# Hybrid decoder step on one core: retention state updates whose operands are stacked on TensorE, with cross products gathered in one tile and new states made in rounds

## The chip, the cores and the metric

One core of one Trainium2 chip runs the whole layer in one launch. The metric is the device time of that launch in microseconds (us), the median of several runs. TensorE (PE in the profile) multiplies matrices, PEld is its loading of weights, DVE is VectorE, ACT is ScalarE, POOL is GpSimd and SP is the engine that issues most loads.

## What is computed

One layer of a hybrid decoder works on 256 prompt tokens of one sequence and on 8 new tokens of each of 8 sample sequences (320 tokens in all, width 2048, float32). The lines that matter here are those of the retention mixer, per head (4 heads, 256 wide), for the sample sequences:

```
scores  = einsum('bhid,bhjd->bhij', q, k) * decay          # new tokens among themselves
o_inner = einsum('bhij,bhje->bhie', scores, v)
o_cross = einsum('bhid,bhde->bhie', q, S) * q_dec          # new tokens against the old state
S_new   = gamma**C * S + einsum('bhjd,bhje->bhde', k * k_dec, v)
```

S is a 256 x 256 state for each of 8 sequences and 4 heads. C is 8 for the sample sequences. A pooling mixer, an output projection and a SwiGLU feed-forward network follow. Outputs are y for all tokens and the new states.

## The kernel before

All activations are kept transposed (features on partitions, 320 tokens along the free axis). A float32 product is made of float32r products: each operand is split into a high part (a ScalarE cast, L152) and a low part (a VectorE subtraction, L155), and three products are summed (L160 hi*hi, L161, L162). `project` runs one projection of 16 feature tiles by 4 output blocks: 192 matmuls of 128x320 into four PSUM accumulators (`acc_...` in the profile). For each head there are two projections (`acc_qk`, `acc_vg`), then come two for the pooling mixer (`acc_u`), four for the output (`acc_wo`) and those of the feed-forward network (`acc_gu`, `acc_dn`).

Between the matmuls of a projection stand the small stages of a head: transposes (`tps`, `tpk`, `tvs`, `tpv`), scores (`sc`, `scs`), outputs (`o`), cross products with the old state (`cr`, L418), the final prompt state (`st`), new sample states (`ns`, L538), sample outputs (`os`, L552 and L553) and the gate (`on`). They take PSUM from a pool of three banks (`aux`). A list scheduler fixes each engine's order when the program is built, and each engine then runs its own instructions in that order.

For the samples of a head the new k and v (64 tokens on 64 partitions) are split into halves in `smp`. A state update of the sequence pair `bp` wants a stack of 32 rows (high and low halves of k against those of v, for 8 tokens) on its own quarter of the partitions, `kv[32*bp : 32*bp + 32]`. Before, this was made by a trip through DRAM: four writes of `smp` to `kv_d` and four loads of `kv` on POOL's queue. Then `new_state(bp)` makes four matmuls with 32 contraction rows (two sequences `b`, two halves `t`) and VectorE adds the decayed state (L541). The cross products `cr` write 16 partitions for each pair; a ScalarE scaling, a write to `x_d` and one load bring them together in `cx`, which `sample_outputs` multiplies by a 0/1 table `sel`. The other product of `sample_outputs` has 64 contraction rows (`vs_f`, `sds`).

Of the kernel before, what the change touches and what calls it, by code (L numbers as in the profile page):

```python
# [24 lines left out]
P = 128  # L25
# [37 lines left out]
N_CON = _at  # L63


def _constants():
# [12 lines left out]
    i = np.arange(TP)[None, :]  # L79
    for h in range(H):  # L80
        mask[h, :, P:] = np.where(i >= j, np.exp((i - j) * lg[h]), 0.0) * ks
        a = CON["mask_s"][0] + TS * h
        sj = np.arange(TS)[:, None]
        si = np.arange(TS)[None, :]
        ok = (sj % NB == si % NB) & (si >= sj)
        con[:TS, a : a + TS] = np.where(ok, np.exp((si - sj) // NB * lg[h]), 0.0) * ks
        for t in range(2):
            con[:, CON["kdec"][0] + 2 * h + t] = np.exp((TP - 1 - (np.arange(P) + P * t)) * lg[h]) * ks
        con[:TS, CON["kdec_s"][0] + h] = np.exp((NS - 1 - np.arange(TS) // NB) * lg[h]) * ks
        con[:16, CON["qdec"][0] + h] = np.exp((np.arange(16) % NS + 1) * lg[h])  # L90
# [6 lines left out]
    return trig, con.astype(f32), mask.astype(f32), decay  # L97
# [3 lines left out]
def layer_kernel(ctx, tc, x, vec, trig, con, mask, pool_in, s_ret, w_in, w_pool, w_out, w_gu, w_dn,  # L101
# [7 lines left out]
    dram = ctx.enter_context(tc.tile_pool(name="dram", bufs=4, space=bass.MemoryType.DRAM))  # L109
# [170 lines left out]
    with ExitStack() as ret_ctx:  # L280
# [129 lines left out]
        def cross(h, bp, q_s, x_d):  # L410
# [4 lines left out]
            for b in range(2):  # L415
                for t in range(2):
                    for n_, s_ in enumerate((lo, hi)):
                        nc.tensor.matmul(ps[:16, b * DK : b * DK + DK],  # L418
                                         q_s[:, t, 2 * bp + b].rearrange("p s j -> p (s j)"),
                                         s_[:, b, t * DK : t * DK + DK],  # L420
                                         start=t == 0 and n_ == 0, stop=t == 1 and n_ == 1)
            cr = rp.tile([16, 2, DK], F32, tag="cr", name=f"cr_sb{h}_{bp}")
            nc.scalar.mul(cr, ps[:16].rearrange("p (b e) -> p b e", b=2), cst("qdec", h, 1, 16))
            nc.gpsimd.dma_start(out=x_d[2 * bp : 2 * bp + 2].rearrange("b r e -> r b e"), in_=cr)

        def head(h, accs_qk, project_vg):
# [7 lines left out]
            x_d = dram.tile([NB, 16, DK], F32, tag="x_d", name=f"x_d{h}")  # L434
            kv_d = dram.tile([4, NS, NB, 2, DK], F32R, tag="kv_d", name=f"kv_d{h}")
            smp = rp.tile([TS, 2, 2, DK], F32R, tag="smp", name=f"smp{h}")
            ktok = keep.tile([P, 2, 2, DK], F32R, tag="ktok", name=f"ktok{h}")
            q_s = rp.tile([P, 2, NB, 2, NS], F32R, tag="q_s", name=f"q_s{h}")
# [3 lines left out]
            sds = rp.tile([TS, TS], F32, tag="sds", name=f"sds{h}")  # L442
# [22 lines left out]
            def k_sample():  # L465
# [3 lines left out]
                split2_scaled(smp[:, 1, 0], smp[:, 1, 1], ps[:TS, :DK], cst("kdec_s", h, 1, TS))  # L469
                for t in range(2):  # L470
                    qt = q_r[:, t, TP:].rearrange("p (j b) -> p b j", b=NB)
                    split2(q_s[:, t, :, 0], q_s[:, t, :, 1], qt)

            def sample_scores():
# [20 lines left out]
            vs_f = rp.tile([TS, DK], F32, tag="vs_f", name=f"vs_f{h}")  # L495
            o_t = t640(f"o_t{h}")
            kv = rp.tile([P, 2, 2, DK], F32R, tag="kv", name=f"kv{h}")

            def v_sample():
# [3 lines left out]
                nc.vector.tensor_copy(vs_f, ps[:TS, :DK])  # L503
# [7 lines left out]
            def kv_load(bp):  # L511

                nc.gpsimd.dma_start(out=kv[32 * bp : 32 * bp + 32],
                                    in_=kv_d.rearrange("q j b a e -> (q j) b a e")[:, 2 * bp : 2 * bp + 2])
# [18 lines left out]
            def new_state(bp):  # L533
                raw, ks = s_raws.pop(4 * h + bp), slice(32 * bp, 32 * bp + 32)
                for b in range(2):
                    ps = aux(f"ns{h}_{bp}_{b}")
# [4 lines left out]
                    nc.vector.scalar_tensor_tensor(sl, sl, decay[h], ps.rearrange("p (t e) -> p t e", t=2),  # L541
                                                   op0=ALU.mult, op1=ALU.add)
                nc.gpsimd.dma_start(out=o_rs[h, bp], in_=raw)
                s_load(4 * h + bp + 4)

            def sample_outputs():
                cx = rp.tile([P, DK], F32, tag="cx", name=f"cx{h}")
                nc.gpsimd.dma_start(out=cx, in_=x_d.rearrange("b r e -> (b r) e"))
# [5 lines left out]
                nc.scalar.copy(o_t[:, :, TP:], ps[:, : 2 * TS].rearrange("p (e t) -> p e t", e=2))  # L554
# [387 lines left out]
```

## Time and profile before

| | |
|---|---|
| three runs | 1435.94, 1436.27 (median), 1436.89 us |
| the profiled execution's own time | 1435.48 us |
| its span, first to last instruction | 1433.7 us |
| PE busy | 1409.2 us, 98% |
| DVE busy | 751.5 us, 52% |
| ACT busy | 578.5 us, 40% |
| POOL busy | 63.6 us, 4% |

The span and the 1.8 us around it make the profiled execution's time. A matmul's listed duration is longer than its distance to the next one, since matmuls overlap in the array; what a matmul costs TensorE is read from start to start.

### The profile page before, as it was taken

How to read it: one execution, taken by the hardware profiler on the slowest of the kernel's cores; microseconds unless marked ns; L12 is line 12 of the kernel's file. 1: busy time of each engine (PE TensorE's matmuls, PEld its weight loads, DVE VectorE, ACT ScalarE, POOL GpSimd, SP SyncE). 2: the span in 40 equal slices, each digit the busy share in tenths (PEclk: the TensorE clock that was granted, in tenths of full speed). 3: DMA queues.
4: the chain of work that ended last, by engine and by line, in shares of the span. 5: the costliest groups of instructions: out<-in, count | busy, mean ns of one | idle time of the engine just before them, and what ended most of it. 6: DMA issues, size and time to landing. Idle time of an engine off the chain costs nothing.

```text
span 1433.7 us, 22936 instructions
## 1 busy us (share of the span) xinstructions
PE 1409.2 (98%) x9578; PEld 1390.9 (97%) x9578; DVE 751.5 (52%) x1003; ACT 578.5 (40%) x751; POOL 63.6 (4%) x122
## 2 busy tenths in 40 slices
PE   8999999999999999999999999999999999999995
PEld 8999999999999989999999999999999999999995
DVE  7657575758644674444334444444544444454455
ACT  6445454545444353333333333223333323333352
POOL 1020202021000000000000000000000000000000
PEclk9999999999999999999999999999999999999998
DMA  9484747575564145544444444444454444444442
GB/s 335 134 258 145 237 166 239 169 237 159 173 235 150 57 148 170 156 153 153 148 148 147 150 148 158 148 147 149 151 155 149 147 147 153 153 149 148 147 133 74
DMA packets 69368, 233.84 MB, mean 163 GB/s; under 512 B 8368, under 2 KB 10864, under 8 KB 69264
## 3 DMA queue, kind: packets, MB, share of 16 engines
q1 hardware_dynamic: 58608, 204.28, 44.5%
q0 software_dynamic: 10080, 27.44, 6.1%
q8 instruction: 75, 1.23, 0.3%
q10 hardware_dynamic: 576, 0.66, 0.1%
q14 instruction: 29, 0.24, 0.0%
HBM read 216.28 MB, written 16.05 MB: 162 GB/s over the span
## 4 chain that ended last, share of the span: by engine, by line
PE 95%; DVE 3%; ACT 1%; DMA 0%; issue 0%; DVEq 0%; ACTq 0%; POOLq 0%
PE acc_gu L162 14%; PE acc_gu L160 14%; PE acc_gu L161 14%; PE acc_dn L160 7%; PE acc_dn L162 7%; PE acc_dn L161 7%; PE acc_vg L161 3%; PE acc_vg L162 3%; PE acc_wo L162 3%; PE acc_vg L160 3%; PE acc_wo L161 3%; PE acc_wo L160 3%; PE acc_qk L160 3%; PE acc_qk L161 3%; PE acc_qk L162 2%; PE acc_u L160 1%
## 5 line engine op out<-in xcount | busy, mean ns | idle before, releaser
L160 PE MATMUL acc_gu<-hf_h,hi_gu 128*128 128x320 f32 x1312 | 405.5, 309 | 0.2 <-ACT hi_gu L152 0.2
L161 PE MATMUL acc_gu<-hf_l,hi_gu 128*128 128x320 f32 x1312 | 405.1, 309 | 0.0
L162 PE MATMUL acc_gu<-hf_h,lo_gu 128*128 128x320 f32 x1312 | 403.0, 309 | 1.9 <-DVE lo_gu L155 1.9
L155 DVE TENSOR_TENSOR lo_gu<-raw_gu,hi_gu 128x1024 fp32r<-128x1024 f32 x166 | 203.1, 1223 | 270.3 <-ACT hi_gu L152 270.3
L152 ACT CAST hi_gu<-raw_gu 128x1024 fp32r<-128x1024 f32 x166 | 174.1, 1049 | 336.2 <-PE acc_gu L161 300.1
L162 PEld LDWEIGHTS acc_gu<-hf_h,lo_gu 128*128 128x128 f32 x1312 | 245.6, 188 | 2.7 <-DVE lo_gu L155 2.7
L160 PEld LDWEIGHTS acc_gu<-hf_h,hi_gu 128*128 128x128 f32 x1312 | 246.3, 188 | 0.6 <-ACT hi_gu L152 0.5
L161 PEld LDWEIGHTS acc_gu<-hf_l,hi_gu 128*128 128x128 f32 x1312 | 246.3, 188 | 0.1
L161 PE MATMUL acc_dn<-a_l,hi_dn 128*128 128x320 f32 x704 | 217.3, 309 | 0.0
L160 PE MATMUL acc_dn<-a_h,hi_dn 128*128 128x320 f32 x704 | 217.3, 309 | 0.0
L162 PE MATMUL acc_dn<-a_h,lo_dn 128*128 128x320 f32 x704 | 215.4, 309 | 0.0
L155 DVE TENSOR_TENSOR lo_dn<-raw_dn,hi_dn 128x1024 fp32r<-128x1024 f32 x88 | 107.7, 1224 | 137.8 <-ACT hi_dn L152 137.7
L152 ACT CAST hi_dn<-raw_dn 128x1024 fp32r<-128x1024 f32 x88 | 92.2, 1048 | 183.0 <-PE acc_dn L161 153.3
L160 PEld LDWEIGHTS acc_dn<-a_h,hi_dn 128*128 128x128 f32 x704 | 132.2, 188 | 0.0
L161 PEld LDWEIGHTS acc_dn<-a_l,hi_dn 128*128 128x128 f32 x704 | 132.2, 188 | 0.0
L162 PEld LDWEIGHTS acc_dn<-a_h,lo_dn 128*128 128x128 f32 x704 | 131.6, 188 | 0.0
L152 ACT CAST hi_in<-raw_in 128x1024 fp32r<-128x1024 f32 (+1 forms) x82 | 83.8, 1026 | 96.9 <-PE acc_qk L161 48.4
L155 DVE TENSOR_TENSOR lo_in<-raw_in,hi_in 128x1024 fp32r<-128x1024 f32 (+1 forms) x82 | 97.7, 1194 | 46.4 <-ACT hi_in L152 45.4
L161 PE MATMUL acc_vg<-xw_l,hi_in 128*128 128x320 f32 x256 | 79.8, 312 | 0.0
L161 PE MATMUL acc_wo<-mi_l,hi_wo 128*128 128x320 f32 x256 | 79.0, 309 | 0.0
L160 PE MATMUL acc_vg<-xw_h,hi_in 128*128 128x320 f32 x256 | 78.8, 310 | 0.0
L162 PE MATMUL acc_vg<-xw_h,lo_in 128*128 128x320 f32 x256 | 78.7, 309 | 0.0
(351 smaller groups left out, 2057.0 us busy)
## 6 DMA issues: line engine op xcount, KB each, us to landing
raw_gu<-in_w_gu SPq DMA_DIRECT2D x168, 512.0 KB, 3.5
raw_dn<-in_w_dn SPq DMA_DIRECT2D x88, 512.0 KB, 3.6
raw_in<-in_w_in SPq DMA_DIRECT2D x78, 512.0 KB, 4.4
raw_wo<-in_w_out SPq DMA_DIRECT2D x32, 512.0 KB, 3.6
s_raw<-in_s_ret POOLq DMA_DIRECT2D x16, 512.0 KB, 5.8
out_rs<-s_raw POOLq DMA_DIRECT2D x16, 512.0 KB, 5.4
x_t<-in_x SPq DMA_DIRECT2D x8, 320.0 KB, 4.0
kv_d<-smp POOLq DMA_DIRECT2D x16, 128.0 KB, 4.9
```

The costliest lines, as they stand in the source:

```text
L152: nc.scalar.copy(hi[:, ks], src[:, ks])
L155: nc.vector.tensor_tensor(lo[:, ks], src[:, ks], hi[:, ks].bitcast(F32), op=ALU.subtract)
L160: nc.tensor.matmul(ps, wh, xh, start=start, stop=False)
L161: nc.tensor.matmul(ps, wh, xl, start=False, stop=False)
L162: nc.tensor.matmul(ps, wl, xh, start=False, stop=stop)
```

## The change

- `smp` now holds the high halves on partitions 0 to 63 and the low halves on 64 to 127. The new function `stacked` multiplies it by a 0/1 table `part` (two matmuls for k, two for v), and ScalarE copies the result to `kv`. `kv_d`, its writes and its loads are gone. The table (256 KB) is loaded by SP at the start and cast by ScalarE once.
- `cross` writes 32 partitions of one PSUM tile for a pair (the stationary q gets zero columns for the other sequence), and ScalarE scales it straight into its quarter of `cx`. `x_d`, its writes and the load of `cx` are gone.
- `vs_f` and `sds` have 128 partitions, the upper 64 zero, so all four products of `sample_outputs` have 128 contraction rows.
- `new_states` replaces `new_state`: a round takes up to three (pair, sequence) items with a PSUM bank for each, and issues the `t=0` products of all of them, then the `t=1` products. The first product of a round waits by an added dependency for the last two evictions ahead of it. Three rounds for a head: sequence 0 of pairs 0 to 2, sequence 1 of pairs 0 to 2, both sequences of pair 3. Sample outputs and gate stand between the rounds; the prompt's final state comes last.
- `vs_f`, `q_s`, `sds` become tiles for the whole run, cleared by three VectorE memsets at the start.

```diff
+    part = np.zeros((P, 2, 2, P), f32)
+    for a in range(2):
+        low = r // (NS << a) % 2
+        for b in range(2):
+            part[TS * low + r % NS * NB + r // 32 * 2 + b, a, b, r] = 1.0
...
+    vs_f = keep.tile([P, DK], F32, name="vs_f")
+    nc.vector.memset(vs_f, 0.0)
+    q_s = keep.tile([P, 2, 4, 4, 2, NS], F32R, name="q_s")
+    nc.vector.memset(q_s.bitcast(F32), 0.0)
+    part = keep.tile([P, 2, 2, P], F32R, name="part")
+    sds = keep.tile([P, TS], F32, name="sds")
+    nc.vector.memset(sds, 0.0)
...
-                        nc.tensor.matmul(ps[:16, b * DK : b * DK + DK],
-                                         q_s[:, t, 2 * bp + b].rearrange("p s j -> p (s j)"),
+                        nc.tensor.matmul(ps[:32, :DK],
+                                         q_s[:, t, bp, 2 * b : 2 * b + 2].rearrange("p c s j -> p (c s j)"),
                                          s_[:, b, t * DK : t * DK + DK],
-                                         start=t == 0 and n_ == 0, stop=t == 1 and n_ == 1)
-            cr = rp.tile([16, 2, DK], F32, tag="cr", name=f"cr_sb{h}_{bp}")
-            nc.scalar.mul(cr, ps[:16].rearrange("p (b e) -> p b e", b=2), cst("qdec", h, 1, 16))
-            nc.gpsimd.dma_start(out=x_d[2 * bp : 2 * bp + 2].rearrange("b r e -> r b e"), in_=cr)
+                                         start=b + t + n_ == 0, stop=b + t + n_ == 3)
+            nc.scalar.mul(cx[32 * bp : 32 * bp + 32], ps[:32, :DK], cst("qdec", h, 1, 32))
+        def stacked(kv, a, smp, name):
+            ps = aux(f"tp{'vk'[a]}r{name}")
+            for b in range(2):
+                nc.tensor.matmul(ps[:, b * DK : b * DK + DK], part[:, a, b], smp[:, a], start=True, stop=True)
+            nc.scalar.copy(kv[:, :, a], ps.rearrange("p (b e) -> p b e", b=2))
...
-                split2(smp[:, 0, 0], smp[:, 0, 1], ps[:TS, :DK])
-                for q in range(4):
-                    both = smp.rearrange("p a s e -> p (a s) e")[:, q % 2 : 3 + q // 2 : 2 + q // 2 - q % 2]
-                    nc.gpsimd.dma_start(out=kv_d[q].rearrange("j b a e -> (j b) a e"), in_=both)
-                for bp in range(4):
-                    kv_load(bp)
+                split2(smp[:TS, 0], smp[TS:, 0], ps[:TS, :DK])
...
+            def new_states(some):
+                pss = [aux(f"ns{h}_{bp}_{b}") for bp, b in some]
+                def product(i, t):
+                    (bp, b), ps = some[i], pss[i]
+                    ks = slice(32 * bp, 32 * bp + 32)
+                    return nc.tensor.matmul(ps[:, t * DK : t * DK + DK], kv[ks, b, 1, t * P : t * P + P],
+                                            kv[ks, b, 0, :], start=True, stop=True).ins
+                i0 = 0 if evicted else len(some) - 1
+                start = product(i0, 0)
+                for e in evicted[-2:]:
+                    tc.add_manual_dep(start, e.name, SYNC, reason="a round at a time")
+                with tc.issue_after(start):
+                    for t in range(2):
+                        for i in range(len(some)):
+                            if t or i != i0:
+                                product(i, t)
...
+            rounds = [[(bp, 0) for bp in range(3)], [(bp, 1) for bp in range(3)], [(3, 0), (3, 1)]]
...
-            return [v_sample, v_tokens, outputs] + state + [lambda: cross(h, 3, q_s, x_d)] + [
-                lambda bp=bp: new_state(bp) for bp in range(4)] + [sample_outputs, gate]
+            return [v_sample, v_tokens, v_stacked, outputs, lambda: cross(h, 3, cx), lambda: new_states(rounds[0]),
+                    sample_outputs, lambda: new_states(rounds[1]), gate, lambda: new_states(rounds[2])] + state
```

What the scheduler makes of it is seen on TensorE in head 0, where the new states stand among the matmuls of head 1's `acc_qk` (192 in all). In `ns_2_0_1025` the first number is the pair, the second the sequence, and the third only a buffer number. Before:

```order
L538 MATMUL ns_0_0_1043<-kv_851 128x256 x2
L538 MATMUL ns_0_1_1047<-kv_851 128x256 x2
L538 MATMUL ns_1_0_1054<-kv_851 128x256 x2
...
L538 MATMUL ns_1_1_1058<-kv_851 128x256 x2
...
L538 MATMUL ns_2_0_1095<-kv_851 128x256 x2
...
L538 MATMUL ns_2_1_1099<-kv_851 128x256 x2
...
L538 MATMUL ns_3_0_1136<-kv_851 128x256 x2
L538 MATMUL ns_3_1_1140<-kv_851 128x256 x2
L160 MATMUL acc_qk_0_852<-xw_h,hi_in_4_969 128x320
```

And now, the first two rounds with the sample outputs between them:

```order
L550 MATMUL ns_2_0_1025<-kv_501 128x256
L550 MATMUL ns_0_0_1023<-kv_501 128x256
L550 MATMUL ns_1_0_1024<-kv_501 128x256
L550 MATMUL ns_0_0_1023<-kv_501 128x256
L550 MATMUL ns_1_0_1024<-kv_501 128x256
L550 MATMUL ns_2_0_1025<-kv_501 128x256
...
L577 MATMUL os_1035<-sds,vs_f 128x64
L578 MATMUL os_1035<-con_t,cx_500 128x64
L577 MATMUL os_1035<-sds,vs_f 128x64
L578 MATMUL os_1035<-con_t,cx_500 128x64
...
L550 MATMUL ns_0_1_1071<-kv_501 128x256
```

Five groups of `ns`, after 96, 118, 121, 123 and 144 matmuls of the projection, have become three, after 96, 142 and 173, with four products of pair 3 in the last. The sample outputs moved from 145 to 120, the gate's `on` from 177 to 166. The new `stacked` products for v stand after 67 (the transposes that feed them after 26), those for k after 104 of `acc_vg`. In heads 1 to 3 the counts are nearly the same; in head 3 before, the new states stood in seven groups instead of five, and in the pooling stage `pp_0` moved from 133 to 151 matmuls into the second `acc_u`.

On VectorE in head 0, from the split of the new v on, the rows were these before:

```order
L404 TENSOR_TENSOR smp_495<-tvs_886,smp_495 64x256
L155 TENSOR_TENSOR lo_s_3_998<-s_raw_504,hi_s_3_997 128x1024
L155 TENSOR_TENSOR lo_in_5_1016<-raw_in_5_856,hi_in_5_1015 128x1024
L155 TENSOR_TENSOR lo_in_6_1068<-raw_in_6_907,hi_in_6_1067 128x1024
L541 SCALAR_TENSOR_TENSOR s_raw_312<-s_raw_312,ns_0_0_1043 128x512
L541 SCALAR_TENSOR_TENSOR s_raw_312<-s_raw_312,ns_0_1_1047 128x512
L541 SCALAR_TENSOR_TENSOR s_raw_350<-s_raw_350,ns_1_0_1054 128x512
```

They are now, up to the second round's evictions:

```order
L565 SCALAR_TENSOR_TENSOR s_raw_319<-s_raw_319,ns_0_0_1023 128x512
L565 SCALAR_TENSOR_TENSOR s_raw_357<-s_raw_357,ns_1_0_1024 128x512
L565 SCALAR_TENSOR_TENSOR s_raw_507<-s_raw_507,ns_2_0_1025 128x512
L167 TENSOR_TENSOR lo_in_7_1095<-raw_in_7_949,hi_in_7_1094 128x1024
L167 TENSOR_TENSOR lo_in_0_1153<-raw_in_0_993,hi_in_0_1152 128x1024
L277 SCALAR_TENSOR_TENSOR osq_1122<-osq_1122 128x320
L565 SCALAR_TENSOR_TENSOR s_raw_319<-s_raw_319,ns_0_1_1071 128x512
L565 SCALAR_TENSOR_TENSOR s_raw_357<-s_raw_357,ns_1_1_1072 128x512
L565 SCALAR_TENSOR_TENSOR s_raw_507<-s_raw_507,ns_2_1_1073 128x512
```

The evictions (one for each sequence and pair, as before) now come three at a time, and the second three stand behind the first step of the gate (`osq`).

## Rows read from the trace of the kernel before

**Rows 1.** The page: busy time, share and instructions of each engine.
```profile
PE 1409.2 (98%) x9578; PEld 1390.9 (97%) x9578; DVE 751.5 (52%) x1003; ACT 578.5 (40%) x751; POOL 63.6 (4%) x122
```

**Rows 2.** Stretches: span, busy by engine (instructions), TensorE clock, DMA share, GB/s.
```profile
8.08:11.49 3.41, 3.14 (x12) 3.14 (x13) 3.41 (x8) 2.46 (x4) 0.00 (x0) 0.50 1.00 396
118.00:190.00 72.00, 72.00 (x500) 68.88 (x499) 46.05 (x68) 34.42 (x44) 12.57 (x23) 1.00 0.63 201
321.80:346.00 24.20, 24.20 (x166) 24.04 (x165) 24.05 (x44) 11.07 (x20) 3.24 (x6) 1.00 0.50 155
```

**Rows 3.** Timeline of PE, head 0: start, length (us), instruction.
```profile
87.78 0.31 PE L160 MATMUL acc_qk<-xw_h,hi_in 128*128 128x320 f32 x1
...
90.27 0.31 PE L162 MATMUL acc_qk<-xw_h,lo_in 128*128 128x320 f32 x1
90.51 0.74 PE L538 MATMUL ns<-kv 32*128 32x256 f32 x6
...
91.43 0.31 PE L161 MATMUL acc_qk<-xw_l,hi_in 128*128 128x320 f32 x1
...
94.36 0.31 PE L160 MATMUL acc_qk<-xw_h,hi_in 128*128 128x320 f32 x1
94.60 0.50 PE L538 MATMUL ns<-kv 32*128 32x256 f32 x2
...
95.28 0.31 PE L162 MATMUL acc_qk<-xw_h,lo_in 128*128 128x320 f32 x1
...
100.05 0.31 PE L162 MATMUL acc_qk<-xw_h,lo_in 128*128 128x320 f32 x1
100.29 0.74 PE L538 MATMUL ns<-kv 32*128 32x256 f32 x4
...
101.30 0.43 PE L552 MATMUL os<-sds,vs_f 64*128 64x64 f32 x2
...
102.39 0.43 PE L553 MATMUL os<-con_t,cx 128*128 128x64 f32 x2
...
102.87 0.31 PE L162 MATMUL acc_qk<-xw_h,lo_in 128*128 128x320 f32 x1
```

**Rows 4.** Timeline of PE, head 3, in its sample outputs.
```profile
317.20 0.33 PE L553 MATMUL os<-con_t,cx 128*128 128x64 f32 x2
317.46 0.43 PE L552 MATMUL os<-sds,vs_f 64*128 64x64 f32 x2
```

**Rows 5.** The chain that ended last: start, share of the chain (us), what.
```profile
76.10 0.44 PE tpv L520 x4
86.13 0.93 PE cr L418 x8
```

**Rows 6.** Tiles `ns`, `smp`, `lo_in` on DVE: duration ns min/median/max, first and last start (us).
```profile
L541 DVE SCALAR_TENSOR_TENSOR s_raw<-s_raw,ns x32: 679/686/690, 91.0 to 314.6; 128x512 f32<-128x512 f32 x32
...
L404 DVE TENSOR_TENSOR smp<-tvs,smp x4: 406/406/408, 79.1 to 293.9; 64x256 fp32r<-64x256 f32 x4
...
L155 DVE TENSOR_TENSOR lo_in<-raw_in,hi_in x82: 681/1220/1226, 7.6 to 340.5; 128x1024 fp32r<-128x1024 f32 x78, 128x512 fp32r<-128x512 f32 x4
```

**Rows 7.** Timeline of PE and DVE at the start.
```profile
1.06 3.76 PE L139 MATMUL warm_first<-ones 128*128 128x128 f32 x16 [1.06 <-DVE eps_t L119]
6.37 0.82 PE L166 MATMUL acc_qk<-xw_h,hi_in 128*128 128x320 f32 x4 [1.55 <-DVE xw_h L316]
...
0.84 0.17 DVE L117 MEMSET ones<- 128x128 f32 x1 [0.84 <-PEq L920]
```

**Rows 8.** ACT by groups, 70 to 190 us: form xcount | busy, mean ns | idle before, by whom.
```profile
L152 ACT CAST hi_in<-raw_in 128x1024 fp32r<-128x1024 f32 x27 | 28.1, 1045 | 33.8 <-PE acc_qk L161 27.6 <-PE acc_vg L161 3.7 <-issue 2.3
...
L423 ACT ACTIVATE cr_sb<-cr,con_t 16x512 f32<-16x512 f32 x6 | 4.1, 677 | 2.3 <-PE cr L418 2.1
L587 ACT COPY st_sb<-st 128x512 f32<-128x512 f32 x2 | 1.2, 588 | 1.7 <-PE st L162 0.8 <-DMA kv_d<-smp 0.8
...
L554 ACT COPY o_t<-os 128x128 f32<-128x128 f32 x2 | 0.5, 267 | 3.1 <-PE os L553 3.1
```

More of the change, by code (lines that the diff above doesn't have):

```diff
@@ L63 @@
 N_CON = _at
+SYNC = mybir.DependencyInfo(mybir.DependencyClass.Sync, mybir.DependencyReason.DATA)
 def _constants():
@@ L433, in head @@
                     nc.sync.dma_start(out=msk, in_=mask[h])
-            x_d = dram.tile([NB, 16, DK], F32, tag="x_d", name=f"x_d{h}")
-            kv_d = dram.tile([4, NS, NB, 2, DK], F32R, tag="kv_d", name=f"kv_d{h}")
-            smp = rp.tile([TS, 2, 2, DK], F32R, tag="smp", name=f"smp{h}")
+            cx = rp.tile([P, DK], F32, tag="cx", name=f"cx{h}")
+            kv = rp.tile([P, 2, 2, DK], F32R, tag="kv", name=f"kv{h}")
+            smp = rp.tile([P, 2, DK], F32R, tag="smp", name=f"smp{h}")
             ktok = keep.tile([P, 2, 2, DK], F32R, tag="ktok", name=f"ktok{h}")
-            q_s = rp.tile([P, 2, NB, 2, NS], F32R, tag="q_s", name=f"q_s{h}")
             sd = rp.tile([P, 2, TP], F32, tag="st", name=f"sd{h}")
@@ L441, in head @@
             sd_l = rp.tile([P, 2, TP], F32R, tag="sd_l", name=f"sd_l{h}")
-            sds = rp.tile([TS, TS], F32, tag="sds", name=f"sds{h}")
             def k_tokens():
@@ L483, in head @@
                 s_load(3)
-            accs = project_vg([k_sample, k_tokens, scores, sample_scores] +
-                              [lambda bp=bp: cross(h, bp, q_s, x_d) for bp in range(3)])
+            if h == 0:
+                nc.scalar.copy(part, late.pop("part").rearrange("p (a b r) -> p a b r", a=2, b=2))
+            accs = project_vg([k_sample, k_tokens, scores, sample_scores, lambda: stacked(kv, 1, smp, f"{h}")] +
+                              [lambda bp=bp: cross(h, bp, cx) for bp in range(3)])
             v_t = t640(f"v_t{h}")
@@ L502, in v_sample @@
                     nc.tensor.transpose(ps[:TS, e * P : e * P + P], v_t[:, e, TP:T], ident)
[L503 to L514 removed]
+                nc.vector.tensor_copy(vs_f[:TS], ps[:TS, :DK])
+                split2(smp[:TS, 0], smp[TS:, 0], ps[:TS, :DK])
             def v_tokens():
@@ L531, in outputs @@
                 nc.scalar.copy(o_t[:, :, :TP], po.rearrange("p (e t) -> p e t", e=2))
[L533 to L536, printed above, removed]
-                    for t in range(2):
-                        nc.tensor.matmul(ps[:, t * DK : t * DK + DK], kv[ks, b, 1, t * P : t * P + P], kv[ks, b, 0, :],
-                                         start=True, stop=True)
-                    sl = raw[:, 2 * b : 2 * b + 2, :]
[L541 to L544, printed above, removed]
+            evicted = []
@@ new lines, in new_states @@
+            def new_states(some):
[10 more added lines that the diff above has]
+                with tc.issue_after(start):
+                    for t in range(2):
+                        for i in range(len(some)):
+                            if t or i != i0:
+                                product(i, t)
+                for (bp, b), ps in zip(some, pss):
+                    raw = s_raws[4 * h + bp]
+                    sl = raw[:, 2 * b : 2 * b + 2, :]
+                    evicted.append(nc.vector.scalar_tensor_tensor(
+                        sl, sl, decay[h], ps.rearrange("p (t e) -> p t e", t=2), op0=ALU.mult, op1=ALU.add).ins)
+                    if b:
+                        nc.gpsimd.dma_start(out=o_rs[h, bp], in_=s_raws.pop(4 * h + bp))
+                        s_load(4 * h + bp + 4)
@@ L546, in sample_outputs @@
+            rounds = [[(bp, 0) for bp in range(3)], [(bp, 1) for bp in range(3)], [(3, 0), (3, 1)]]
             def sample_outputs():
-                cx = rp.tile([P, DK], F32, tag="cx", name=f"cx{h}")
-                nc.gpsimd.dma_start(out=cx, in_=x_d.rearrange("b r e -> (b r) e"))
                 ps = aux(f"os{h}")
@@ L553, in sample_outputs @@
                     nc.tensor.matmul(ps[:, e * TS : e * TS + TS], cx[:, es], cst("sel", 0, TS), start=False, stop=True)
-                nc.scalar.copy(o_t[:, :, TP:], ps[:, : 2 * TS].rearrange("p (e t) -> p e t", e=2))
+                evicted.append(nc.scalar.copy(o_t[:, :, TP:], ps[:, : 2 * TS].rearrange("p (e t) -> p e t", e=2)).ins)
             def gate():
@@ L572, in head, with v_stacked @@
             state = [lambda: final_state(h, ktok, vtok, rp)()] if h < H - 1 else []
-            return [v_sample, v_tokens, outputs] + state + [lambda: cross(h, 3, q_s, x_d)] + [
-                lambda bp=bp: new_state(bp) for bp in range(4)] + [sample_outputs, gate]
+            def v_stacked():
+                stacked(kv, 0, smp, f"{h}")
+            return [v_sample, v_tokens, v_stacked, outputs, lambda: cross(h, 3, cx), lambda: new_states(rounds[0]),
+                    sample_outputs, lambda: new_states(rounds[1]), gate, lambda: new_states(rounds[2])] + state
         def final_state(h, ktok, vtok, pool):
@@ L666, in tables @@
         def tables():
+            late["part"] = t640("part_raw").rearrange("p a t -> p (a t)")[:, : 4 * P]
             with tc.issue_after(at["last"].ins):
                 nc.sync.dma_start(out=con_t, in_=con)
+                nc.sync.dma_start(out=late["part"], in_=part_in)
         p_state = {}
```

23 lines of the change are left out of this document (10 added, 13 removed).

## The prediction

> **What bounds the kernel now.** I read the busy line of the page first, then the stretches, then PE's timeline at each small stage. PE is busy for 98% of the span, DVE for 52% [rows 1]. A mean over stages does not say that PE sets the pace in the heads, so I cut out one stretch of 72 us about one head long: PE is busy for 72.00 us of it, DVE for 46.05, ACT for 34.42, at a granted clock of 1.00 [rows 2]. No engine keeps PE waiting there. From 8.35 us to the end of the pooling mixer PE's list holds no idle time, so a microsecond less of PE work in the heads is a microsecond at the end, unless a new wait takes it.
>
> What a small stage costs PE is not its listed length. Between 87.78 and 90.27 stand 17 matmuls: (90.27 - 87.78) / 17 = 0.1465 us from start to start [rows 3]. A visit of a small stage costs what the starts of the projection's matmuls around it lie apart, less 0.1465 for each of those matmuls. (The listed starts are those of the last one ahead and the second one behind, since the first one behind is drawn out.)
>
> **What the new states and sample outputs cost before.** From [rows 3]:
> - six `ns` products in one visit: 91.43 - 90.27 - 0.293 = 0.87 us;
> - two: 95.28 - 94.36 - 0.293 = 0.63;
> - four, one matmul of the projection, then the eight records of `os`: 102.87 - 100.05 - 0.44 = 2.38.
>
> Six and four products have the same listed length, 0.74. The last two of the six lie on another quarter of the rows than the four ahead of them, so they ran beside them. Four products alone thus cost 0.87 too, and the sample outputs 2.38 - 0.87 = 1.51. Heads 0 to 2 have one visit of six, three of two, one of four: 0.87 + 3 x 0.63 + 0.87 + 1.51 = 5.14. Head 3 had seven groups, one of four and six of two: 0.87 + 6 x 0.63 + 1.51 = 6.16 (its sample outputs stand in two pieces; I give them the same 1.51). In all 3 x 5.14 + 6.16 = 21.6 us.
>
> Of the 0.63, two products at 0.117 each (eight products of the same 256 columns took 0.93 as `cr` [rows 5]) are 0.23. The other 0.4 is what going into and out of 32-row products costs beyond the matmuls. So fewer visits matter more than fewer products.
>
> **What they cost after.** A round of three items issues three products on three quarters, then three more. If the three run side by side, a round is as long as two products: 0.63. If not at all, four products come on top: 0.63 + 4 x 0.117 = 1.1. I take 0.65, near the lower end, since the six of before are the same case with two quarters and showed no cost. The third round has all four on one quarter: 0.87. The sample outputs lose their 64-row form. Eight records at the pace of full transposes, 0.44 / 4 = 0.11 [rows 5], are 0.88; I take 0.90. The bounds: a pair of `con_t` records behind a full-row matmul takes 317.46 - 317.20 = 0.26 with one change of form behind it [rows 4], and the 64-row pairs follow each other at (102.39 - 101.30) / 3 = 0.363 with a change between each [rows 3]. Four pairs at 0.16 are 0.64 (0.10 for the change taken off, an estimate from 0.363 against 0.26), four at 0.26 are 1.06. The `stacked` products are new: four of 256 columns, 4 x 0.117 = 0.47 for a head, at full rows without a change of form. Their bounds are nothing below 0.4 (columns alone) and 0.9 if each visit drew out a neighbour by 0.2.
>
> Sum for a head: 0.65 + 0.65 + 0.87 + 0.90 + 0.47 = 3.54; four heads, 14.2. The saving is 21.6 - 14.2 = **7.4 us**.
>
> A rule speaks against full overlap. The Trainium skill (TensorE: Matmul & The Clock Gate, Part 3: Packing small matmuls) gives four row tiles a measured speedup of 3.07, not 4. Three tiles would by that estimate take some 0.2 of a product more a step, 16 steps in all: 0.4 us less saved, 1429.3 for the forecast below. The trace's equal 0.74 speaks for no such loss with two. The Trainium skill (TensorEngine Tiling (Array Packing), Key Properties) says that changing the tiling mode drains TensorE; the 0.4 us of [rows 3] agrees with it, and by it every visit saved counts.
>
> **What I cost at nothing, and its cover.**
> - The DRAM trips of `kv`, `cr` and `cx` (POOL issues them): no wait of PE on them stands in the trace, so nothing comes back.
> - `cr` has 32 instead of 16 stationary columns: its pace goes by the streamed 256, so 0.93 stays.
> - ACT: `cr` scaled for 512 columns, 0.68, becomes 256 columns; two copies of `kv`, 0.59 each by the copy of the same shape, are new [rows 8]: +2 x 0.59 - 4 x 0.2 = +0.4 us for a head on an engine busy for 34 of 72 us, whose casts wait for PE, not the other way.
> - DVE: the same eviction for each sequence, 0.69 [rows 6].
> - The loads: 256 KB of table on SP ahead of later tiles of x, and the pool state on POOL. PE's waits at the start name DVE (`xw_h`, `lo_in`) [rows 7].
> - Three memsets ahead of `ones`: 256, 512 and 64 columns at 0.17 for 128 [rows 7] are 1.1 us on DVE. `warm_first` starts at 2.2 instead of 1.06 and ends at 5.9 instead of 4.8. The first product starts at 6.37, by DVE's `xw_h`, so 0.45 is left.
>
> **Waits that the new order adds, and their slack** (matmuls in between from the order, at 0.1465):
> - Sample outputs stand 24 matmuls, 3.5 us, behind round one, whose banks DVE must free: 3 x 0.69 = 2.1, or 3.3 with one `lo_in` of 1.22 [rows 6] ahead.
> - Round two stands 22 matmuls, 3.2 us, behind them; ACT's copy is 0.27 and a cast ahead of it 1.05 [rows 8].
> - Round three stands 31 matmuls and the gate behind, 4.5 us or more. DVE's three evictions stand behind `osq` and its sequel: 3.3 again with one `lo_in`.
> - `stacked` for v stands 41 matmuls, 6.0 us, behind its transposes. Before, the low half of v was written at 79.1 + 0.41 [rows 6], 3.4 us after `tpv` at 76.1 [rows 5]: 2.6 left.
>
> All fit, by 0.2, 1.9, 1.2 and 2.6 us. If a round came late, what stands behind it on PE is all of the projection.
>
> **The forecast.** The profiled execution took 1435.48: the span of 1433.7 and 1.8 around it. It lies 0.8 under the median of the runs. 1435.48 - 7.4 = 1428.1; with 0.8 back, **1428.9 us**.
>
> **The rivals.**
> - *Quarters do not overlap.* Eight rounds at 1.1 instead of 0.65 give back 3.6 us: 1432.5. For it: three need three banks written at once, which the trace never shows. Against: the equal 0.74.
> - *A round waits (the other side).* Each `ns` round and `os` now starts behind an eviction of the stage just ahead. Twelve such starts; the gain is gone at 7.4 / 12 = 0.62 us each, and at (7.4 + 2.9) / 12 = 0.86 the kernel is slower beyond what can be told. It would happen if two `lo_in` (2.4 us) stood ahead of three evictions: 4.5 us against 3.5, 1 us at each start: 1428.9 + 12 = 1441. Against: DVE is idle for 26 of 72 us [rows 2].
> - *Head 3's gain is lost.* In the stretch 321.8 to 346 DVE is busy for 24.05 of 24.20 us [rows 2], with the pooling's work. If PE, there earlier by 2.6 us, must wait for DVE, head 3's 6.16 - 3.54 = 2.6 us are lost: 1431.5. Against: PE is as full there, and the sums of DVE are cut off from PE by many matmuls.
> - *The start moves.* In 8.08 to 11.49 PE works at 0.50, the 1.2 GHz level, behind a stretch from 4.82, the end of `warm_first`, in which it ran for 0.82 us [rows 2, 7]. If `warm_first`, 1.1 us later, lies closer to the first products, the 1.7 us that the lower level costs there (half of 3.4) may shrink or another such stretch may come: 1427.2 or 1430.6.
> - *The change doesn't do what it says:* visits split up in other heads, or `os` keeps its 1.3 to 1.5. That is 2 to 3 us back: 1431.
>
> **How the numbers follow.** Forecast (with the start's shift either way) 0.66, no overlap 0.10, head 3 lost 0.07, visits not merged 0.07, waits 0.10, of these half above 1439. Below 1425.8 would need both the faster start and `os` at its lower bound; 1433 takes in the first, third and fifth rival. 0.2%, 2.9 us, is about what a measurement tells from no change. Faster means under 1433.4: all but the waits and a bit of the no-overlap case, 0.87. Same 0.07, slower 0.06.
>
> **What would show it.** Right: PE's timeline in heads 0 to 3 has three `ns` groups, those of six as long as before's groups of two (0.50); eight `os` records without a 64-row form in about 0.9; two `stacked` pairs of 0.23; PE's list of waits has no `ns`, `os` or `tpvr`; PE busy near 1402. Wrong: groups of six near 0.9 or longer; waits of PE for the evictions (`s_raw`) or `o_t`; a changed length of the stretch at 0.50; a gain that is there at the end of head 3 and gone by the start of `acc_wo`.

## The result and the profile after

| | before | now |
|---|---|---|
| median of four runs | 1436.43 us | 1428.26 us (1427.9 to 1428.6) |
| the profiled execution's own time | 1435.48 us | 1427.90 us |
| its span | 1433.7 us | 1426.1 us |

The ratio of the times is 0.9944, with a 95% interval of 0.9932 to 0.9956. The change made the kernel faster, and the time stands 0.6 us from the predicted 1428.9.

The page's busy line answers to [rows 1], the stretches to [rows 2] (the same columns):

```profile
PE 1401.0 (98%) x9594; PEld 1389.6 (97%) x9594; DVE 752.2 (53%) x1006; ACT 581.5 (41%) x760; POOL 35.4 (2%) x70
```

```profile
8.08:11.49 3.41, 2.74 (x10) 2.74 (x11) 3.41 (x9) 1.63 (x3) 0.00 (x0) 0.54 1.04 412
118.00:190.00 72.00, 72.00 (x518) 70.35 (x517) 47.66 (x69) 35.75 (x47) 5.56 (x10) 1.00 0.58 186
321.80:346.00 24.20, 24.20 (x167) 24.20 (x166) 20.81 (x36) 11.55 (x17) 1.13 (x3) 1.00 0.56 169
```

PE still fills the 72 us in the heads, but now with 518 instructions instead of 500. Its busy time fell by 8.2 us, to 1401.0. POOL's nearly halved (63.6 to 35.4, 122 to 70 instructions): the trips through DRAM are gone. That is worth nothing by itself, since no wait of PE hung on them before.

PE's timeline, the start and head 0 (it answers to [rows 3, 4, 7]):

```profile
1.94 3.46 PE L151 MATMUL warm_first<-ones 128*128 128x128 f32 x16 [1.94 <-DVE eps_t L131]
6.77 0.82 PE L178 MATMUL acc_qk<-xw_h,hi_in 128*128 128x320 f32 x4 [1.37 <-DVE xw_h L328]
...
56.41 0.31 PE L173 MATMUL acc_vg<-xw_l,hi_in 128*128 128x320 f32 x1
56.56 0.40 PE L442 MATMUL tpkr<-smp,part 128*128 128x256 f32 x2
...
56.95 0.31 PE L172 MATMUL acc_vg<-xw_h,hi_in 128*128 128x320 f32 x1
...
89.58 0.31 PE L174 MATMUL acc_qk<-xw_h,lo_in 128*128 128x320 f32 x1
89.81 0.51 PE L550 MATMUL ns<-kv 32*128 32x256 f32 x6
...
90.50 0.31 PE L173 MATMUL acc_qk<-xw_l,hi_in 128*128 128x320 f32 x1
...
93.73 0.31 PE L174 MATMUL acc_qk<-xw_h,lo_in 128*128 128x320 f32 x1
93.88 0.33 PE L577 MATMUL os<-sds,vs_f 128*128 128x64 f32 x2
...
94.92 0.31 PE L173 MATMUL acc_qk<-xw_l,hi_in 128*128 128x320 f32 x1
...
103.56 0.31 PE L173 MATMUL acc_qk<-xw_l,hi_in 128*128 128x320 f32 x1
103.80 0.73 PE L550 MATMUL ns<-kv 32*128 32x256 f32 x4
...
104.71 0.31 PE L172 MATMUL acc_qk<-xw_h,hi_in 128*128 128x320 f32 x1
```

A group of six `ns` products is now listed with 0.51 us, as long as a group of two was before (0.50). By the starts around them, as in the prediction: a visit of six costs 90.50 - 89.58 - 0.293 = 0.63 us, the third round 104.71 - 103.56 - 0.293 = 0.86, the sample outputs 94.92 - 93.73 - 0.293 = 0.90, a pair of `stacked` products 56.95 - 56.41 - 0.293 = 0.25.

PE's waits, the whole list (whom it waited for, us in total, times, longest):

```profile
PE warm_first L151 <- DVE eps_t L131: 1.9, 1, 1.9
PE acc_gu L174 <- DVE lo_gu L167: 1.9, 3, 0.7
PE acc_qk L178 <- DVE xw_h L328: 1.4, 1, 1.4
PE acc_gu L178 <- DVE mt L818: 1.3, 2, 1.0
PE acc_qk L179 <- DVE lo_in L167: 1.2, 1, 1.2
PE acc_gu L179 <- DVE lo_gu L167: 0.5, 1, 0.5
PE acc_gu L172 <- ACT hi_gu L164: 0.2, 1, 0.2
```

No `ns`, `os` or `tpvr` is in it. The new order added no wait in the heads.

The lengths of the stages say where the time went. They are differences of the starts of the first matmul of each projection in PE's timeline. Before, at head 1, at the end of head 3's projections and at the feed-forward network:

```profile
70.98 0.31 PE L160 MATMUL acc_qk<-xw_h,hi_in 128*128 128x320 f32 x1
285.96 0.31 PE L160 MATMUL acc_u<-xw_h,hi_in 128*128 128x320 f32 x1
478.13 0.41 PE L166 MATMUL acc_gu<-hf_h,hi_gu 128*128 128x320 f32 x1
```

And now:

```profile
71.52 0.31 PE L172 MATMUL acc_qk<-xw_h,hi_in 128*128 128x320 f32 x1
281.34 0.31 PE L172 MATMUL acc_u<-xw_h,hi_in 128*128 128x320 f32 x1
470.60 0.42 PE L178 MATMUL acc_gu<-hf_h,hi_gu 128*128 128x320 f32 x1
```

| stretch | before | now | difference |
|---|---|---|---|
| start of span to first product | 6.37 | 6.77 | +0.40 |
| first `acc_qk` | 31.89 | 32.07 | +0.18 |
| first `acc_vg` | 32.71 | 32.69 | -0.02 |
| `acc_qk` and `acc_vg` of heads 1, 2, 3, each | 71.66 | 69.94 | -1.72 |
| `acc_u` and `acc_wo` | 192.17 | 189.26 | -2.91 |
| the rest | | | -0.1 |

In all: 0.56 - 3 x 1.72 - 2.91 = -7.5 us. (`acc_wo` itself starts 9.3 us earlier; 1.8 of these are a stage of the pooling mixer, `pp`, that now stands among its matmuls.)

The first two projections have to be taken together. Before, the small stage `tot_x` stood behind the last matmul of the first `acc_qk`, and 0.25 us of what it drew out fell to `acc_vg`; now it stands 13 matmuls ahead. Together the two took 0.16 us longer. That is head 0's share of the change: a pair of `stacked` products (0.24) less three visits of `cr`, each 0.03 shorter. So the stages of the four heads gained 3 x 1.72 + 2.91 - 0.16 = 7.9 us, and the first product came 0.40 later.

VectorE, start and head 0:

```profile
6.24 0.39 DVE L328 TENSOR_SCALAR xw_h<-xt,vec_t 128x320 fp32r<-128x320 f32 x1 [4.34 <-DMA vec_t<-in_vec]
...
90.36 1.88 DVE L565 SCALAR_TENSOR_TENSOR s_raw<-s_raw,ns 128x512 f32<-128x512 f32 x3 [1.09 <-PE ns L550]
...
95.00 1.23 DVE L167 TENSOR_TENSOR lo_in<-raw_in,hi_in 128x1024 fp32r<-128x1024 f32 x1 [1.63 <-ACT hi_in L164]
```

Three evictions take 1.88 us and end at 92.24; the sample outputs begin at 93.88. Behind one more `lo_in` DVE idles for 1.63 us.

### The profile page after: what moved, and what is told of

Read it like the earlier page. It is cut to its first block, busy times and chain, and to the rows that moved or that the text cites. A ratio compares the mean times of both kernels' runs of the same rounds, so it can differ in the third digit from the quotient of the medians.

```text
span 1426.1 us, 22873 instructions
## 1 busy us (share of the span) xinstructions
PE 1401.0 (98%) x9594; PEld 1389.6 (97%) x9594; DVE 752.2 (53%) x1006; ACT 581.5 (41%) x760; POOL 35.4 (2%) x70
## 4 chain that ended last, share of the span: by engine, by line
PE 95%; DVE 3%; ACT 1%; DMA 0%; issue 0%; DVEq 0%; ACTq 0%; POOLq 0%
PE acc_gu L174 14%; PE acc_gu L172 14%; PE acc_gu L173 14%; PE acc_dn L174 7%; PE acc_dn L172 7%; PE acc_dn L173 7%; PE acc_vg L172 3%; PE acc_wo L172 3%; PE acc_vg L174 3%; PE acc_wo L174 3%; PE acc_vg L173 3%; PE acc_wo L173 3%; PE acc_qk L172 3%; PE acc_qk L174 3%; PE acc_qk L173 3%; PE acc_u L172 1%
```

## The experiments

Theory: TensorE sets the pace from the first projection to the end. A visit (one small stage between two matmuls of the projection) of 32-row products costs 0.39 us for going in and out, and 0.117 for each step on its fullest quarter (a quarter is 32 partitions, the fullest holds most of the visit's products, and a step is one of them behind another). So the gain is that of fewer visits and fuller rounds, plus that of full-row sample outputs, less 0.48 us a head for the stacking. Rivals: the gain comes from the removed DRAM trips; or the quarters do not overlap freely; or the new order lives on thin slack; or the start moved.

**e1: the rounds undone.**

```diff
-rounds = [[(bp, 0) for bp in range(3)], [(bp, 1) for bp in range(3)], [(3, 0), (3, 1)]]
+rounds = [[(bp, 0), (bp, 1)] for bp in range(4)]
...
-        sample_outputs, lambda: new_states(rounds[1]), gate, lambda: new_states(rounds[2])] + state
+        sample_outputs, lambda: new_states(rounds[1]), lambda: new_states(rounds[2]), gate, lambda: new_states(rounds[3])] + state
```

> The changed kernel with its rounds undone: four groups of one pair each (both sequences on one quarter); the stacked products, the gathered cross products and the full-row sample outputs stay. TensorE's order then has, for a head, two visits of two products and three of four, where the changed kernel has two of six and one of four. Theory (a visit costs 0.39 us for going into and out of 32-row products, and 0.117 us for each product that has no neighbour on another quarter): 2 x 0.63 + 3 x 0.86 = 3.84 us against 2 x 0.63 + 0.86 = 2.12, so +1.7 us for a head and +6.9 in all, about 1435. Rival (the gain is that of the removed DRAM trips and not of the rounds): within 1 us of the changed kernel's 1428.3.

Measured: 1435.39 us, ratio to before 0.9991 (0.9982 to 1.0). Without the rounds nearly all of the gain is gone, though the trips stay removed. Each of heads 1 to 3 took 71.64 us, +1.70 against the changed kernel, and `acc_u` with `acc_wo` +1.71: 6.8 us, where 6.9 was expected. The profiled execution lost 1.4 us more at the start, in its first `acc_qk` (33.45 us, see the last section).

**e2: item by item inside a round.**

```diff
-for t in range(2):
-    for i in range(len(some)):
-        if t or i != i0:
-            product(i, t)
+product(i0, 1)
+for i in range(len(some)):
+    if i != i0:
+        product(i, 0)
+        product(i, 1)
```

> The changed kernel with the six products of a round issued item by item (both halves of one quarter, then of the next) instead of one half of all three quarters and then the other half. Theory of the prediction (quarters run beside each other whatever the order, as the six products of before did): a visit of six stays at 0.63 us, 1428.3 within 0.7. Rival (products start in order, so that two of one quarter hold back the next quarter): four steps instead of two, 0.63 + 2 x 0.117 = 0.87 us, eight visits, +1.9 us, about 1430.2.

Measured: 1427.84 us, ratio 0.9941 (0.9926 to 0.9956). PE's timeline, a round of six:

```profile
89.64 0.31 PE L174 MATMUL acc_qk<-xw_h,lo_in 128*128 128x320 f32 x1
89.88 0.51 PE L550 MATMUL ns<-kv 32*128 32x256 f32 x6
...
90.57 0.31 PE L173 MATMUL acc_qk<-xw_l,hi_in 128*128 128x320 f32 x1
```

90.57 - 89.64 - 0.293 = 0.64 us, and heads of 69.93. The quarters run beside each other in either order; the order in which halves and items are issued makes next to no difference.

**e3: 64-row sample outputs.**

```diff
-nc.tensor.matmul(ps[:, e * TS : e * TS + TS], vs_f[:, es], sds, start=True, stop=False)
+nc.tensor.matmul(ps[:, e * TS : e * TS + TS], vs_f[:TS, es], sds[:TS], start=True, stop=False)
```

> The changed kernel with the new tokens' product of the sample outputs on 64 contraction rows again (the zero rows of its two operands are left out of it); the order of every engine is the same. Theory (the alternation of 64-row and 128-row products costs 1.51 - 0.89 = 0.6 us for a head): +2.5 us, about 1430.8. Rival (the full-row form saves nothing, the sample outputs were cheaper only for their place): no change.

Measured: 1430.65 us, ratio 0.9959 (0.9945 to 0.9973). Heads of 70.55, +0.61 each. PE's timeline:

```profile
93.50 0.31 PE L174 MATMUL acc_qk<-xw_h,lo_in 128*128 128x320 f32 x1
93.73 0.43 PE L577 MATMUL os<-sds,vs_f 64*128 64x64 f32 x2
...
95.30 0.31 PE L173 MATMUL acc_qk<-xw_l,hi_in 128*128 128x320 f32 x1
```

95.30 - 93.50 - 0.293 = 1.51 us, as worked out for before. With every engine's order unchanged, this is the form of the products alone: zeros on 64 more rows save a head 0.61 us, where four changes of form fall away.

**e4: the pool state's load held back at the start.**

```diff
-nc.gpsimd.dma_start(out=p_state[g], in_=pool_in[...])
+with tc.issue_after(at["last"].ins):
+    nc.gpsimd.dma_start(out=p_state[g], in_=pool_in[...])
```

> The changed kernel with the load of the pool state held back behind the weights loads of the second half of the heads, as the kernel before had it, instead of at the start; the three memsets at the start stay. Theory (its 120 KB share POOL's queue with the vector table at the start, which landed 0.4 us later than before): the first product starts at 6.37 us again instead of 6.77, -0.4 us, about 1427.9. Rival (the memsets, or chance from run to run, made the start late): the first product stays near 6.8 us, no change.

Measured: 1428.57 us, ratio 0.9948 (0.9933 to 0.9963). The edit missed: POOL's timeline still has the load at 2.14 us. Yet the vector table was there by 5.78 and the first product started at 6.31. So with the load in its place the table can land as early as before, and the 0.40 us of the table above can't be laid to it. Seven more kernels with the same start (e1 to e3, e5, e7, e9, e10) started between 6.28 and 6.65. What moves it from run to run is not settled.

**e5: the rounds dealt out anew.** The third round gets two quarters instead of one.

```diff
-rounds = [[(bp, 0) for bp in range(3)], [(bp, 1) for bp in range(3)], [(3, 0), (3, 1)]]
+rounds = [[(0, 0), (1, 0), (2, 0)], [(3, 0), (0, 1), (1, 1)], [(2, 1), (3, 1)]]
```

> The changed kernel with the rounds dealt out anew: (pair, sequence) 00 10 20, then 30 01 11, then 21 31, so that the third round has two quarters instead of one. Theory (0.39 us for a visit and 0.117 for each step on the fullest quarter): the third round falls from 0.86 to 0.63 us, four heads, -0.9 us, about 1427.4. Rival (a round of four is paced by its four banks' halves or its issue, not by the quarters): no change, 1428.3.

Measured: 1426.7 us, ratio 0.9929 (0.9915 to 0.9944). PE's timeline, the third round:

```profile
101.78 0.31 PE L173 MATMUL acc_qk<-xw_l,hi_in 128*128 128x320 f32 x1
102.01 0.50 PE L550 MATMUL ns<-kv 32*128 32x256 f32 x4
...
102.70 0.31 PE L172 MATMUL acc_qk<-xw_h,hi_in 128*128 128x320 f32 x1
```

102.70 - 101.78 - 0.293 = 0.63 us, and heads of 69.71: -0.23 each, 0.9 us in four. The profiled execution gained 1.8 more at the start, by a shorter first `acc_qk` (30.72 us) and an earlier first product.

**e6: stacking by the DRAM trip again.** The `stacked` products, their copies and the table are out; for k and v:

```diff
+for q in range(4):
+    both = smp.rearrange("p a s e -> p (a s) e")[:, q % 2 : 3 + q // 2 : 2 + q // 2 - q % 2]
+    nc.gpsimd.dma_start(out=kv_d[q].rearrange("j b a e -> (j b) a e"), in_=both)
+for bp in range(4):
+    nc.gpsimd.dma_start(out=kv[32 * bp : 32 * bp + 32], in_=kv_d...[:, 2 * bp : 2 * bp + 2])
```

> The changed kernel with the stacking on TensorE undone alone: the split of k and v goes through DRAM to its quarters as in the kernel before (four writes and four loads a head on POOL's queue), and the table's load, its cast and the stacked products and copies are gone; rounds, gathered cross products and full-row sample outputs stay. Theory (the trips were hidden, and the stacking costs TensorE 0.48 us a head): -1.9 us, about 1426.3, no wait of TensorE for kv. Rival (with rounds in the place of single pairs the loads land too late, or cost by contention what they save): TensorE waits for kv ahead of the first round, 1 us or more a head, 1429 to 1433.

Measured: 1431.31 us, ratio 0.9957 (0.9942 to 0.9972); the six times lie between 1426.61 and 1433.70. In the profiled execution (1432.08) heads 1 to 3 took 69.47, -0.47 each, as the theory has it, and the first `acc_qk` took 33.43, 1.4 more than in the changed kernel. In head 3 the rival came true. PE's timeline there, and the landing of the sixteen loads of `kv`, in this run and in the kernel before:

```profile
303.40 0.69 PE L555 MATMUL ns<-kv 32*128 32x256 f32 x6 [2.99 <-DMA kv<-kv_d]
...
304.87 0.47 PE L174 MATMUL acc_u<-xw_h,lo_in 128*128 128x320 f32 x1
305.13 0.47 PE L172 MATMUL acc_u<-xw_h,hi_in 128*128 128x320 f32 x1
```

```profile
DMA to landing us min/median/max: 2.7/2.9/6.4
```

```profile
DMA to landing us min/median/max: 2.7/2.9/3.2
```

A load lands 2.9 us after its issue in the median, but 6.4 at worst, and the round waits for the last of three. The third was issued at 296.93, at the same time as a 512 KB load of weights (296.92), and landed at 303.35. After 3 us, at 299.9, it would have been there 0.5 us before TensorE was, at 300.41. In the kernel before, no load of `kv` took more than 3.2 us, and the first product of each head started 1.4 to 2.4 us after its load had landed. That the load of weights delayed this one is the likely reading; no run separates the two. After the 3.0 us wait 12 matmuls of the projection ran at 0.27 instead of 0.1465 us from start to start (granted clock 0.50 from 304.9 to 308.2 us), which costs 1.4 more. The stacking costs TensorE 1.9 us and buys the end of that risk.

**e7: stacked products twice.** The loop over the two `stacked` products stands twice.

> The changed kernel with every stacked product issued twice into the same place (same values). Theory (TensorE sets the pace in the heads, so 4 x 0.117 us more work a head is at the end in full): +1.9 us, about 1430.2. Rival (TensorE's time there is partly covered by another engine's pace): well under 1 us more.

Measured: 1429.59 us, ratio 0.9952 (0.9937 to 0.9967). Heads of 70.41: +0.47 each, 4 x 0.117, in full. Of the 1.9 us in the stages the medians show 1.3. (The profiled execution's first product started 0.5 us earlier than that of the changed kernel, which hides part of it in the time.)

**e8: e5 and e6 together.**

> The two edits of the runs beside it together: rounds dealt 00 10 20, 30 01 11, 21 31, and k and v stacked by the trip through DRAM. Theory (both save TensorE work, and the sums add): -0.9 - 1.9 = -2.8 us, about 1425.5, below both kernels. Rival (the loads land late, so that the first round of a head waits): no better than the deal of the rounds alone, 1427 or more.

Measured: 1426.16 us, ratio 0.9925 (0.9909 to 0.9942), with times of 1425.51, 1426.04, 1426.28 and 1431.48. The profiled execution is the one of 1431.48. PE's list has the wait again, in three of four heads (in total, times, longest):

```profile
PE ns L555 <- DMA kv<-kv_d: 3.4, 3, 1.8
```

Where the loads land in time the sum holds (the stretch of head 2's tail took 69.24, -0.70); where they don't, all is given back. Here, too, the clock fell, behind the wait of 1.81 us in head 0: it was granted at 0.50 from 95.4 to 98.8 us.

**e9: every eviction twice.**

```diff
+evicted[-1] = nc.vector.scalar_tensor_tensor(
+    sl, sl, decay[h], ps.rearrange("p (t e) -> p t e", t=2), op0=ALU.mult, op1=ALU.add).ins
```

> The changed kernel with each of the eight evictions of a head done twice on VectorE (so the new states and what follows from them are not the reference's): a round of three takes 3.8 instead of 1.9 us of VectorE. Theory (what stands on TensorE behind a round waits for the first bank only, and the next round starts 7.6 us later, so the slack is above 2 us everywhere): no wait of TensorE in the heads, 1428.3 within 1 us. Rival (the other side of the prediction, with a slack of 0.2 us behind the first round): the sample outputs and the rounds wait by 0.4 us or more each, +4 us or more, and a fall of the clock where the wait is long.

Measured: 1428.01 us, ratio 0.9945 (0.993 to 0.996), no wait of PE in the heads. VectorE, round one:

```profile
89.87 1.88 DVE L565 SCALAR_TENSOR_TENSOR s_raw<-s_raw,ns 128x512 f32<-128x512 f32 x3 [1.09 <-PE ns L550]
...
92.81 1.88 DVE L567 SCALAR_TENSOR_TENSOR s_raw<-s_raw,ns 128x512 f32<-128x512 f32 x3
```

The evictions end 2.4 us later, and still nothing waits; heads took 70.03, 0.10 more. The scheduler took part in this: it put the sample outputs later (96.47 instead of 93.88), so the run shows that the order can absorb twice the evictions, not that the fixed order could.

**e10: cross products on 16 columns.**

```diff
-nc.tensor.matmul(ps[:32, :DK], q_s[:, t, bp, 2 * b : 2 * b + 2].rearrange("p c s j -> p (c s j)"),
-                 s_[:, b, t * DK : t * DK + DK], start=b + t + n_ == 0, stop=b + t + n_ == 3)
+nc.tensor.matmul(ps[:16, b * DK : b * DK + DK], q_s[:, t, bp, 3 * b].rearrange("p s j -> p (s j)"),
+                 s_[:, b, t * DK : t * DK + DK], start=t + n_ == 0, stop=t + n_ == 2)
...
```

> The changed kernel with cross products on 16 stationary columns again, a sum of its own for each sequence, of which only the first goes on to the sample outputs (the second sequence's part is left out). In the trace of the changed kernel a visit of eight cross products costs 0.907 us, before 0.935. Theory (the 32 columns, with the sum over both sequences in one place, are what made it shorter): 0.93 again, 16 visits, +0.45 us. Rival (the neighbours made it shorter): 0.907 stays.

Measured, one run: 1428.46 us. The chains of the changed kernel (first row) and of this one (second) have for eight products:

```profile
60.04 0.91 PE cr L431 x8
```

```profile
60.02 0.93 PE cr L431 x8
```

All 16 visits moved that way, by 0.027 us each. Heads of 70.05 are +0.11, four visits' worth.

**e11: k alone by the trip, with e5's rounds.** v stays stacked on TensorE.

```diff
+for q in range(4):
+    nc.gpsimd.dma_start(out=kv_d[q]..., in_=smp[q // 2 * TS : q // 2 * TS + TS, 1])
+for bp in range(4):
+    nc.gpsimd.dma_start(out=kv[32 * bp : 32 * bp + 32, :, 1], in_=kv_d...[:, 2 * bp : 2 * bp + 2])
...
```

> The changed kernel with the rounds dealt 00 10 20, 30 01 11, 21 31, and with k alone stacked by a trip through DRAM (four writes and four loads a head on POOL's queue, issued long before the rounds), v stacked on TensorE as in the changed kernel. Theory (k is ready some 50 us ahead of the first round, so its trip lands in time and 0.24 us of TensorE a head is saved; v's was the late one): against the deal of rounds alone (1426.7) -1.0 us, about 1425.8, no wait for kv. Rival (the trip also loads the queues and delays other loads): a wait of TensorE, or no gain.

Measured: 1425.94 us, ratio 0.9934 (0.9918 to 0.9951). Heads of 69.47, -0.24 against e5, and no wait for `kv`. (The ratio is no better than e5's, since the runs of before beside it were 1 us faster and its own first `acc_qk` took 32.06 us against 30.72.)

**e12: a longer warm-up.**

```diff
-keep_warm(8, "first")
+keep_warm(11, "first")
```

> The changed kernel with 11 instead of 8 warm-up matmuls ahead of the first projection. In the traces so far 0 to 25 of the projection's first 64 matmuls ran at half pace, and the first projection took 30.6 us with none, 32.1 with 10 and 33.4 with 25. Theory (the pause between the warm-up and the first product decides it): the pause is filled, few or no slow matmuls, about -1.5 us, 1426.8. Rival (it is the wait for the first low halves behind the first four products, or chance): 10 or more slow matmuls as before, 1428.3, or later by the warm-up's own overrun of the first product.

Measured: 1426.40 us, ratio 0.9935 (0.992 to 0.9949), and four times within 0.08 us of each other (1426.38 to 1426.46). PE's timeline at the start:

```profile
1.94 5.06 PE L151 MATMUL warm_first<-ones 128*128 128x128 f32 x22 [1.94 <-DVE eps_t L131]
6.66 1.02 PE L178 MATMUL acc_qk<-xw_h,hi_in 128*128 128x320 f32 x4
```

TensorE's list has no wait ahead of the first product any more. Of the first 64 matmuls of the projection 1 ran at half pace, and the first `acc_qk` took 30.64 us instead of 32.07. e11 and e12 touch different places, and all times of each lie below all of the changed kernel's (1427.90 to 1428.60), though the intervals of the ratios overlap. Together they were not run.

## Why the prediction was right, step by step

- **TensorE as the bound, PE time in the heads counted one for one.** Right. e7 added 0.47 us a head, and the stages grew by all of it, 4 x 0.47. (That the medians differ by 1.3 is put down to the start, under e7.)
- **The price of a visit** (0.39 plus 0.117 a step). Right. It gave e1 (6.8 measured, 6.9 expected), e2 and e5. The rounds are worth 6.8 us and the full-row sample outputs 2.4 (e3), less 1.9 for the stacking (e6, e7); the removed DRAM trips are worth nothing.
- **Rounds at 0.65, third round 0.87, sample outputs 0.90, stacking 0.47.** Measured 0.63, 0.86, 0.90 and 0.49: a sum of 3.51 for a head against 3.54. The pace of full transposes gave the right number for `os`, and that may be luck: those records stream 128 columns and those of `os` 64, and no run shows why both take 0.11. e3 shows the 0.61 us of the 64-row form. (Of the bounds written there, four pairs at 0.26 are 1.04, not 1.06.)
- **Overlap of three quarters.** Free to within 0.01 us, in both orders that were run. The Trainium skill (TensorE: Matmul & The Clock Gate, Part 3: Packing small matmuls) says that four row tiles give 3.07 and not 4; by the prediction's estimate from that figure a visit of six would be some 0.05 us longer than one of two. Here both cost 0.63, so the trace does not show such a loss with three quarters.
- **`cr` at 0.93, unchanged.** Off: 0.91. Sixteen visits shorter by 0.026 to 0.028 are 0.4 us of gain that the sum lacks. e10 shows that the 32 columns with the common sum make it, not the neighbours; which of the two does, and why, is open. It is most of why a head gained 1.72 and not 1.60.
- **The start at nothing.** Off in size the other way. The memsets delayed `warm_first` to 1.94, less than the 2.2 worked out, and don't set the first product, as said; but that product came 0.40 later, by the landing of the vector table. It is not shown that the change did this: kernels with the same start had their first product between 6.28 and 6.77. The sum: 7.4 predicted, 7.9 gained in the stages of the heads (0.4 of the difference is `cr`), 0.40 lost at the start, 7.5 net. That the net lies so near 7.4 is luck: two misses of about 0.5 and 0.4 us cancel.
- **The trips and loads at nothing.** Right for before. It holds for that order alone: in e6 the same trips under rounds met late landings and cost a 3.0 us wait.
- **Slack of the new waits.** All held, with more room than worked out. Behind round one the working assumed a `lo_in` ahead of three evictions of 0.69 and left 0.2 us; in the trace the evictions came first, three in 1.88, and left 1.6.
- **The rivals.** No overlap, waits, and visits not merged: none in the trace. Head 3's gain lost: no, `acc_u` and `acc_wo` gave 2.91 and DVE fell from 24.05 to 20.81 us in that stretch (which now holds work of a later stage). The start's clock did not make the difference between the two kernels (11 and 10 slow matmuls), but its size is real between executions: about 1.4 us between the changed kernel and e5, 2.7 between e1 and e5.

## What to carry to other kernels

Where TensorE is the bound, cost a small stage by the starts of its neighbours, not by its own listed length. Leaving and entering a row-tiled form cost more here than the products did (0.39 us against 0.23 for a pair), so gather such products into few visits over different quarters, or pad them with zeros to the full rows. A transfer that hides before may not after the consumers are gathered: a round waits for the last of its loads, and in e6 and e8 an idle TensorE paid again in its clock.

## What was not expected of the hardware

- **The start decides 1 to 3 us.** Counts of slow matmuls (listed with 0.46 us or more instead of 0.31) among the projection's first 64, and the length of the first `acc_qk` (before's lacks 0.25 us of `tot_x`):

| kernel | first product | slow of 64 | first `acc_qk` |
|---|---|---|---|
| e5 | 6.32 | 0 | 30.72 |
| e12 (longer warm-up) | 6.66 | 1 | 30.64 |
| after | 6.77 | 10 | 32.07 |
| before | 6.37 | 11 | 31.89 |
| e7 | 6.28 | 11 | 32.26 |
| e4 | 6.31 | 15 | 32.15 |
| e1 | 6.61 | 25 | 33.45 |

All but before and e12 have the same start in the code. In the changed kernel the stretch from 8.08 to 11.49 us shows a granted clock of 0.54, near the 1.2 GHz level, behind a pause of 1.37 us, four products and another pause of 1.16; in e5 the same stretch shows 1.00, behind pauses of 0.60 and 1.17:

```profile
8.08:11.49 3.41, 3.18 (x22) 3.19 (x23) 3.41 (x8) 1.64 (x3) 0.00 (x0) 1.00 1.04 417
```

Ten to 15 slow matmuls cost about the same, some 1.4 us. DVE is busy for all of these 3.41 us in both. The pauses alone do not decide it: e7 had those of e5 (0.55 and 1.16) and shows 0.65 there. What does is open; e12 shows only that with the first pause filled four times lay at 1426.4.

- **At the very start the pace is the safer reading.** e1's stretch 8 to 11 us shows 1.00, while four matmuls took 1.07 us from start to start there (9.82 to 10.89), nearly twice 4 x 0.1465. The trace's record of the granted clock begins only at 14.6 us in e1, and a stretch ahead of it is printed as 1.00. The pace was half from the first product on and rose when the record begins. In e4 it was the same, up to 11.5 us. The rows are e1's:

```profile
8.00:11.00 3.00, 2.42 (x10) 2.41 (x10) 3.00 (x7) 1.64 (x3) 0.00 (x0) 1.00 1.04 410
```

```profile
9.82 1.27 PE L263 MATMUL acc_qk<-xw_l,hi_in 128*128 128x320 f32 x4
10.89 1.27 PE L178 MATMUL acc_qk<-xw_h,hi_in 128*128 128x320 f32 x4
```

- **A change between 64 and 128 rows costs 0.15 us** (an estimate: a quarter of e3's 0.61 us, all of it put on the four changes), and products on different 32-row quarters overlap in both orders of issue that were run (0.63 us for six, 0.64 in e2).
